# Attention with grouped queries on one core: three of 16 blocks on VectorE in every job from the tenth on

## The chip, the cores and the metric

The kernel runs on one core of a Trainium2 chip. A core has a matrix engine (TensorE, PE in the profile; its weight loads are PEld), a vector engine (VectorE, DVE), a scalar engine for activation functions (ScalarE, ACT), a general engine (GpSimd, POOL) and a queue engine (SyncE, SP). Each runs its own list of instructions in order; semaphores order them against each other. Matmuls write to PSUM, eight banks of 512 fp32 values per partition; tiles in SBUF hold the rest. The metric is the device time of one execution in microseconds (us); lower is better.

## The reference

```python
# Q [8, 512, 32, 64], K and V [8, 512, 8, 64], all fp32
scale = 1.0 / np.sqrt(dim)
K_expanded = np.repeat(K, 4, axis=2)
V_expanded = np.repeat(V, 4, axis=2)
Q, K_expanded, V_expanded = (x.transpose(0, 2, 1, 3) for x in (Q, K_expanded, V_expanded))
scores = np.einsum('bhqd,bhkd->bhqk', Q, K_expanded) * scale
weights = np.exp(scores - np.max(scores, axis=-1, keepdims=True))
weights = weights / (np.sum(weights, axis=-1, keepdims=True) + 1e-10)
output = np.einsum('bhqk,bhkd->bhqd', weights, V_expanded)
return output.transpose(0, 2, 1, 3).astype(np.float32)
```

This is attention of 8 batches, 32 query heads and 8 key heads: four query heads share one key head. Each head's 512 x 512 weights are exponentials of the scores, divided by their row sum.

## The kernel before

**Jobs.** The work is cut into 64 jobs (NJOB), one for each batch and key head, so each job has four query heads: two pairs (NPAIR = 2, index i). Two jobs make a unit u, whose Q is loaded together. The 512 keys are four chunks of 128 (kc), so a job has 2 x 4 x 2 = 16 blocks of 128 keys x 512 queries, numbered by pair, chunk and head of the pair (i, kc, m). Each block goes through scores (keys x queries, TensorE), the exponential, and a second matmul with V (P·V).

**The exponential is shared.** ScalarE does most blocks: `act_tile` takes two blocks at a time, writes their scores with two matmuls (L199) into a two-bank tile s_ps (pool s_pool, two buffers) and reads them with one ACTIVATE (L217) into pt. The other blocks are the first ones of pair 1: `taken(j)` of them, two in a normal job and three in a wide one. `act_tiles` deals the rest out: seven full tiles in a normal job; in a wide one six full tiles and, as the fifth in order (n = 4), a tile with one block, the odd block (half the size).

**The path for VectorE's blocks.** `exp_d` writes their scores into the two banks of d_ps (pool d_pool, one buffer) and VectorE turns them to 16-bit integers u (L228): the exponential's bits as a straight line. `exp_d2` takes the fraction bits f (L249), `exp_d3` computes from them a correction, g (L241) and w (L245), on GpSimd from job 3 to job 62 and on VectorE in the others, and `exp_d4` adds u and w into pt (L262; d4 for short). In a job that follows, d4 is done for the job before: u, f, g and w have two buffers. The third block of a wide job is started at the end of the job before, in the second bank of that job's d_ps tile.

**What else is in a job.** P·V for the job before (L293; `pv`), 32 small matmuls per pair into one PSUM tile pv (one buffer), in pieces between score tiles; `norm` after each pair: a reciprocal of the sums (L336, inv) and a multiply (L340, o_sb), after which pv is free again. The first reciprocal of a job (for pair 0) is called inv0, the second inv1. Eight transposes of the Q of job j + 2 on TensorE into the first bank of a d_ps tile (`trans_q`, L164), and VectorE's copy from there, qt (L167). A check of V's size (`check_v`, L173, okv) in every second job, odd ones up to batch 6 and even ones in batch 7, and a check of the sums (`check_sums`, L304) once in eight jobs. K of the next batch comes transposed through SyncE's queue; Q, K and V are loaded from GpSimd's queue, ahead of g and w in its order.

**The order is written out by hand.** Nothing is scheduled by a planner (`tc.manual_schedule()`); each engine runs its instructions in the order of the loop over j. For a job j in the steady part TensorE has: score tile 0; VectorE's two blocks; score tile 1; P·V of pair 0, 16 matmuls; score tile 2; 16 more; score tile 3; the transposes; score tile 4; P·V of pair 1 up to `cut[0]`; score tile 5; the third block of job j + 1 where that is wide; P·V up to `cut[1]`; score tile 6; the rest of P·V. VectorE has: u; okv; inv0 and multiply; qt; d4 of job j - 1; the sum check; f; u of the third block of j + 1; inv1 and multiply. P·V takes the key chunks in the order 2, 3, 1, 0, so that with three blocks taken the matmuls from the 17th on need d4.

The steps of VectorE's path as the code has them:

```python
nc.vector.tensor_scalar(out=st["u"][:, lo:hi, :], in0=ps[...], scalar1=A_U, scalar2=B_U, ...)
nc.vector.tensor_single_scalar(out=st["f"], in_=st["u"], scalar=1023, op=ALU.bitwise_and)
engine.tensor_scalar(out=g, in0=f, scalar1=-EXP_F1, scalar2=..., op0=ALU.add, op1=ALU.mult)
engine.tensor_tensor(out=w, in0=g, in1=f..., op=ALU.mult)
nc.vector.tensor_tensor(out=st["pt"]..., in0=st["u"], in1=st["w"], op=ALU.add)
```

Of the kernel before, what the change touches and what calls it, by code (L numbers as in the profile page):

```python
# [11 lines left out]
FP32 = mybir.dt.float32  # L12
# [21 lines left out]
V_HI = 1.0e15  # L34


WIDE = lambda j: j >= 10 and j % 2 == 0


@with_exitstack  # L40
# [18 lines left out]
def fast_path(ctx, tc, Q, K, V, out, flag):  # L59
    nc = tc.nc  # L60
    B, S, H, D = Q.shape
# [5 lines left out]
    NPAIR = HPG // 2  # L67
# [16 lines left out]
    s_pool = ctx.enter_context(tc.tile_pool(name="sps", bufs=2, space=PS))  # L84
# [3 lines left out]
    ident = const_pool.tile([128, 128], BF16, name="ident")  # L88
# [9 lines left out]
    kn, qn, kt, qt = {}, {}, {}, {}  # L98

    def load_k(b, lo=0, hi=KV):  # L100
        if b not in kn:
            kn[b] = knat_pool.tile([128, SC, KV, D], BF16, name="k_nat")
        nc.gpsimd.dma_start(  # L103
            out=kn[b][:, :, lo:hi, :],
            in_=K[b, :, lo:hi, :].rearrange("(sc p) g d -> p sc g d", p=128),
        )


    def load_v(b, lo=0, hi=KV, chunks=range(SC)):
        for sc in chunks:  # L110
            nc.gpsimd.dma_start(  # L111
                out=vt[b % 2][:, sc, lo:hi, 0:D],
                in_=V[b, sc * 128:(sc + 1) * 128, lo:hi, :],
            )
# [6 lines left out]
    def load_q(u, cuts=(0, 2 * HPG)):  # L121
        b, gp = divmod(u, GP)
        h0 = gp * 2 * HPG
        qn[u] = qnat_pool.tile([128, SC, 2 * HPG, D], BF16, name="q_nat")
        for lo, hi in zip(cuts[:-1], cuts[1:]):
            nc.gpsimd.dma_start(  # L126
                out=qn[u][:, :, lo:hi, :],
                in_=Q[b, :, h0 + lo:h0 + hi, :].rearrange("(sc p) h d -> p sc h d", p=128),
            )

    def d_tile():
        return d_pool.tile([128, 2, S], FP32, name="d_ps")
# [22 lines left out]
        for to, of in ((0, 64), (64, 0)):  # L155
            nc.sync.dma_start(out=kt[b][to:to + 64, 1, :, :], in_=kt[b][of:of + 64, 0, :, :])

    def trans_q(j, bank, lo=0, hi=NPAIR):
        u, g = divmod(j, 2)
        ps = bank.bitcast(BF16).rearrange("p (i sc c) -> p i sc c", i=NPAIR, sc=SC)  # L160
        for i in range(lo, hi):
            for sc in range(SC):
                h = g * HPG + 2 * i
                nc.tensor.transpose(ps[:, i, sc, :], qn[u][:, sc, h:h + 2, :], ident)  # L164
        if u not in qt:
            qt[u] = qt_pool.tile([128, 2, NPAIR, S], BF16, name="qt")
        return lambda: nc.vector.tensor_copy(  # L167
            out=qt[u][:, g, lo:hi, :], in_=ps[:, lo:hi, :, :].rearrange("p i sc c -> p i (sc c)")
        )

    def check_v(b, sc):
        n = b * SC + sc
        nc.vector.tensor_reduce(  # L173
            out=okv[:, n:n + 1], in_=vt[b % 2][:, sc, :, 0:D], op=ALU.max, axis=AX.XY,
            apply_absolute_value=True,
        )
# [6 lines left out]
    def taken(j):  # L183
        return 3 if WIDE(j) else 2

    def act_tiles(j):
        every = [(i, kc, m) for i in range(NPAIR) for kc in range(SC) for m in range(2)]
        first = DPAIR * SC * 2
        mine = [n for n in range(len(every)) if not first <= n < first + taken(j)]
        groups = [[n for n in mine if n // 2 == h] for h in range(len(every) // 2)]  # L190
        return [[every[n] for n in group] for group in groups if group]
# [3 lines left out]
    def scores(j, ps, i, kc, m):  # L195
        u, g = divmod(j, 2)
        b, gp = divmod(u, GP)
        keys = kt_first[:, gp, :, :] if b == 0 else kt[b][:, :, gp, :]
        nc.tensor.matmul(  # L199
            ps,  # L200
            keys[64 * m:64 * m + 64, g ^ m, kc * 128:(kc + 1) * 128],
            qt[u][64 * m:64 * m + 64, g, i, :],
            start=True,
            stop=True,
        )

    def open_job(j):
        pt = pt_pool.tile([128, NPAIR, SC, 2, S], FP16, name="pt")
        jobs.setdefault(j, {}).update(pt=pt, pv={})

    def act_tile(j, n):
        group = act_tiles(j)[n]
        i, kc, lo = group[0]
        ps = s_pool.tile([128, 2, S], FP32, name="s_ps")
        for _, _, m in group:
            scores(j, ps[:, m, :], i, kc, m)
        nc.scalar.activation(  # L217
            out=jobs[j]["pt"][:, i, kc, lo:, :], in_=ps[:, lo:, :], func=EXP, scale=scale
        )

    def exp_d(j, lo, hi, ps):
        st = jobs.setdefault(j, {})
        if "u" not in st:
            for name, dtype in (("u", I16), ("f", I16), ("g", BF16), ("w", BF16)):
                st[name] = dve_pool.tile([128, 3, S], dtype, name=name + "16")[:, 0:taken(j), :]
        for n in range(lo, hi):
            scores(j, ps[:, n - lo, :], DPAIR, n // 2, n % 2)
        return lambda: nc.vector.tensor_scalar(  # L228
            out=st["u"][:, lo:hi, :], in0=ps[:, 0:hi - lo, :], scalar1=A_U, scalar2=B_U,
            op0=ALU.mult, op1=ALU.add,  # L230
        )


    def by_pool(j):
        return 3 <= j < NJOB - 1
# [11 lines left out]
    def exp_d2(j):  # L247
        st = jobs[j]
        nc.vector.tensor_single_scalar(  # L249
            out=st["f"], in_=st["u"], scalar=1023, op=ALU.bitwise_and  # L250
        )
        if by_pool(j):
            exp_d3(j, nc.gpsimd)

    def exp_d3(j, engine):
        st = jobs[j]
        correction(engine, st["f"], st["g"], st["w"])
# [144 lines left out]
    bank = d_tile()  # L402
    for j in range(8):
        nc.tensor.matmul(bank[:, 1, :], warm[:, 0:128], warm, start=True, stop=True)
    for read in [first_k(0, swap, bank[:, swap, :]) for swap in range(2)]:
        read()
    bank = d_tile()
    trans_q(0, bank[:, 0, :], 0, 1)()


    for j in range(NJOB):
        end = j == NJOB - 1
        last = j - 1
        late = last >= 0
        u, g = divmod(j, 2)
        b, gp = divmod(u, GP)
        open_job(j)
        if j == 1:

            nc.gpsimd.tensor_copy(out=gate, in_=jobs[0]["pt"][0:1, 0, SC - 1, 0, 0:1])  # L420
            load_q(2)
            load_q(3)
        if g == 0 and u >= 1 and u + 3 < NU:
            load_q(u + 3)
        if (gp, g) == (1, 0) and b + 1 < B:
            load_k(b + 1)
        if 3 <= 2 * gp + g < 3 + SC and b + 1 < B:
            load_v(b + 1, chunks=(2 * gp + g - 3,))
        if gp == 2 and g == 0 and b + 1 < B:
            dma_k(b + 1)  # L430

        cut = (4, 18) if taken(j) > 2 else (11, 19)
        act_tile(j, 0)
        if j == 0:
            trans_q(0, bank[:, 1, :], 1, NPAIR)()
            act_tile(j, 1)
            exp_d(j, 0, 2, d_tile())()
        else:
            exp_d(j, 0, 2, d_tile())()
            act_tile(j, 1)  # L440

        if j == 8:
            check_v(0, 0)
        if g == (b < B - 1) and j > 1:
            check_v(b, gp)
        if late:
            pv(last, 0, 0, 16)
        act_tile(j, 2)
        if late:
            pv(last, 0, 16, 32)  # L450
            norm(last, 0)
        act_tile(j, 3)

        reads = []
        if not end:
            bank = d_tile()

            ahead = (j + 1,) if j < 7 else (8, 9) if j == 7 else (j + 2,)
            for n, to in enumerate(ahead):
                if to < NJOB:  # L460
                    reads.append(trans_q(to, bank[:, n, :]))
            if j == 1:
                for swap in range(2):
                    reads.append(first_k(1, swap, bank[:, 1, swap * S // 2:]))
            elif j > 1 and b == 0 and gp + 1 < GP:
                reads.append(first_k(gp + 1, g, bank[:, 1, :]))
        else:
            pv(j, 0, 0, 16)
        for read in reads:
            read()  # L470

        if late and by_pool(last):
            exp_d4(last)
        check_sums()
        exp_d2(j)
        if not by_pool(j):
            exp_d3(j, nc.vector)
            exp_d4(j)
        act_tile(j, 4)
        if late:  # L480
            pv(last, 1, 0, cut[0])
        act_tile(j, 5)
        if not end and taken(j + 1) > 2:
            exp_d(j + 1, 2, taken(j + 1), bank[:, 1:2, :])()
        if late:
            pv(last, 1, *cut)
        act_tile(j, 6)
        if late:
            pv(last, 1, cut[1], 32)
            norm(last, 1)  # L490
            del jobs[last]
        if end:
            pv(j, 0, 16, 32)
            norm(j, 0)
            pv(j, 1, 0, 32)
            norm(j, 1)
# [118 lines left out]
```

## Time and profile before

| what | value |
|---|---|
| median of 3 runs | 423.73 us (423.38 to 423.77) |
| span of the profiled execution, first to last instruction (no other time of it is given) | 422.0 us |
| busy share of that span: PE, PEld, DVE, ACT, POOL | 91%, 55%, 82%, 96%, 69% |
| chain that ended last: ACT, PE, DVE | 54%, 36%, 6% |
| L217, full tile, 421 of them, mean of one | 1086 ns |
| L217, odd block, 27 of them | 753 ns |
| L228, u of two blocks; of one block | 1215 ns; 685 ns |
| L249, f of two blocks; of three | 429 ns; 554 ns |
| L262, d4 of two blocks; of three | 682 ns; 949 ns |
| L241, g on POOL, two blocks; three | 1039 ns; 1466 ns |
| L245, w on POOL, two blocks; three | 2125 ns; 3095 ns |
| POOL's g waiting for DVE's f | 110.1 us, 60 times |
| granted TensorE clock, mean | 0.984 (1.00 in each stage from 20 to 400 us) |

The profile is one execution, taken by the hardware profiler. Times are microseconds from the start of the span. An instruction's duration can overlap the next one's on the same engine, so that rows are best compared by the distances between their starts. A line such as `u<-d_ps` names what is written and what is read; "idle before" and its arrow name the instruction that ended an engine's wait.

### The profile page before, as it was taken

The numbers are of one execution on the slowest core, as the hardware profiler recorded it, in microseconds if no ns is written. First come the engines' busy times: TensorE is split into PE (matmuls) and PEld (weight loads), VectorE is DVE, ScalarE is ACT, GpSimd is POOL, SyncE is SP. The second block draws the span as 40 slices with busy tenths as digits, with TensorE's granted clock in tenths as the row PEclk, the third lists the DMA queues.
The fourth block names the chain that finished last, engine by engine and source line by source line (L and its number), as shares of the span: only waits on it lengthen the run. The fifth ranks groups of instructions, "written<-read, shape, count | busy, mean of one in ns | idle before, by whom it ended". The sixth has DMA issues, their size and how long they took to land.

```text
span 422.0 us, 13063 instructions
## 1 busy us (share of the span) xinstructions
PE 385.7 (91%) x5689; PEld 233.6 (55%) x5689; DVE 344.9 (82%) x611; ACT 404.2 (96%) x449; POOL 291.8 (69%) x209
## 2 busy tenths in 40 slices
PE   6889999999999999999999999999999999999983
PEld 2446565555555555555555555555555555555552
DVE  2697788889888888888888888888989888898875
ACT  3899999999999999999999999999999999999992
POOL 8504656778758876787866887677885887666560
PEclk9599999999999999999999999999999999999998
DMA  9996986599967998499964999649996799642223
GB/s 97 177 139 159 217 165 151 70 207 187 191 151 99 216 198 160 133 198 133 229 150 116 206 163 255 157 69 200 157 225 155 122 206 207 148 123 101 102 91 115
DMA packets 91438, 66.95 MB, mean 159 GB/s; under 512 B 52080, under 2 KB 74608, under 8 KB 91376
## 3 DMA queue, kind: packets, MB, share of 16 engines
q0 software_dynamic: 56544, 25.17, 51.1%
q1 hardware_dynamic: 34832, 40.90, 34.5%
q8 instruction: 45, 0.74, 0.7%
q14 instruction: 17, 0.14, 0.1%
HBM read 50.33 MB, written 33.55 MB: 199 GB/s over the span
## 4 chain that ended last, share of the span: by engine, by line
ACT 54%; PE 36%; DVE 6%; issue 1%; POOL 1%; ACTq 0%; DVEq 0%; POOLq 0%
ACT pt L217 54%; PE s_ps L199 17%; PE pv L293 16%; PE d_ps L199 1%; DVE o_sb L340 1%; PE d_ps L164 1%; DVE pt L262 1%; DVE u L228 1%; DVE qt L167 1%; DVE w L245 0%; POOL q_nat L126 0%; DVE kt_first L146 0%; ACTq L217 0%; PE d_ps L143 0%; DVE f L249 0%
## 5 line engine op out<-in xcount | busy, mean ns | idle before, releaser
L217 ACT ACTIVATE pt<-s_ps 128x1024 f16<-128x1024 f32 (+1 forms) x448 | 402.9, 1066 | 9.1 <-PE s_ps L199 9.0
L293 PEld LDWEIGHTS <-pt 128*128 128x128 f16 x4096 | 144.2, 98 | 86.8 <-issue 50.4
L293 PE MATMUL pv<-v,pt 128*128 128x65 bf16 x4032 | 183.2, 195 | 2.6 <-DVE o_sb L340 1.6
L199 PE MATMUL s_ps<-qt,kt 64*128 64x512 bf16 x757 | 152.7, 384 | 19.9 <-ACT pt L217 15.4
L245 POOL TENSOR_TENSOR w<-g,f 128x1024 bf16<-128x1024 bf16 (+1 forms) x60 | 153.7, 2562 | 5.0
L241 POOL TENSOR_SCALAR g<-f 128x1024 bf16<-128x1024 int16 (+1 forms) x60 | 73.9, 1231 | 110.1 <-DVE f L249 110.1
L228 DVE TENSOR_SCALAR u<-d_ps 128x1024 int16<-128x1024 f32 (+1 forms) x91 | 96.2, 1058 | 1.1 <-PE d_ps L199 1.1
L340 DVE TENSOR_TENSOR o_sb<-pv,inv 128x512 f32<-128x512 f32 x125 | 86.5, 692 | 4.5 <-DVE inv L336 0.2
L199 PEld LDWEIGHTS <-kt 64*128 64x128 bf16 x896 | 49.0, 93 | 62.6 <-issue 35.0
L336 DVE RECIPROCAL inv<-pv 128x8 f32<-128x8 f32 x125 | 25.9, 207 | 55.8 <-PE pv L293 55.4
L262 DVE TENSOR_TENSOR pt<-u,w 128x1536 uint16<-128x1536 int16 (+1 forms) x64 | 50.9, 795 | 0.2
L167 DVE COPY qt<-d_ps 128x1024 bf16<-128x1024 bf16 (+1 forms) x65 | 44.3, 683 | 4.5 <-PE d_ps L164 2.9
L164 PE MATMUL d_ps<-ident,q_nat 128*128 128x128 bf16 x512 | 40.1, 222 | 1.1 <-DVE kt_first L146 0.9
L164 PEld LDWEIGHTS <-q_nat 128*128 128x128 bf16 x512 | 29.2, 98 | 15.8 <-issue 15.7
L199 PE MATMUL d_ps<-qt,kt 64*128 64x512 bf16 x139 | 31.4, 376 | 0.3
L249 DVE TENSOR_SCALAR f<-u 128x1536 int16<-128x1536 int16 (+1 forms) x64 | 30.8, 481 | 0.0
L111 POOL DMA_DIRECT2D v<-in_V_dram x32 | 29.0, 910 | 0.4 <-issue 0.4
L126 POOL DMA_DIRECT2D q_nat<-in_Q_dram x34 | 27.4, 806 | 1.5 <-DMA q_nat<-in_Q_dram 1.3
L199 PE MATMUL s_ps<-qt,kt_first 64*128 64x512 bf16 x112 | 23.7, 419 | 4.1 <-ACT pt L217 3.0
L173 DVE TENSOR_REDUCE okv<-v 128x1 f32<-128x512 bf16 x32 | 21.6, 675 | 0.0
L199 PEld LDWEIGHTS <-kt_first 64*128 64x128 bf16 x128 | 8.0, 95 | 12.2 <-issue 8.4
L103 POOL DMA_DIRECT2D k_nat<-in_K_dram x10 | 7.7, 770 | 1.0 <-POOLq L599 0.8
(40 smaller groups left out, 37.6 us busy)
## 6 DMA issues: line engine op xcount, KB each, us to landing
out_dram<-o_sb SPq DMA_DIRECT2D x31, 1024.0 KB, 6.9
q_nat<-in_Q_dram POOLq DMA_DIRECT2D x31, 512.0 KB, 6.3
k_nat<-in_K_dram POOLq DMA_DIRECT2D x7, 512.0 KB, 8.6
v<-in_V_dram POOLq DMA_DIRECT2D x28, 128.0 KB, 7.6
kt<-kt SPq DMA_DIRECT2D x14, 256.0 KB, 4.6
out_dram<-o_sb SPq DMA_DIRECT2D x4, 256.0 KB, 2.4
kt<-k_nat SPq DMA_TRANSPOSE x28, 5.6
v<-in_V_dram POOLq DMA_DIRECT2D x4, 96.0 KB, 7.8
```

What stands on the lines that cost most here:

```text
L111: nc.gpsimd.dma_start(out=vt[b % 2][:, sc, lo:hi, 0:D], in_=V[b, sc * 128:(sc + 1) * 128, lo:hi, :],)
L164: nc.tensor.transpose(ps[:, i, sc, :], qn[u][:, sc, h:h + 2, :], ident)
L167: return lambda: nc.vector.tensor_copy(out=qt[u][:, g, lo:hi, :], in_=ps[:, lo:hi, :, :].rearrange("p i sc c -> p i (sc c)"))
L199: nc.tensor.matmul(ps, keys[64 * m:64 * m + 64, g ^ m, kc * 128:(kc + 1) * 128], qt[u][64 * m:64 * m + 64, g, i, :], start=True, stop=True,)
L217: nc.scalar.activation(out=jobs[j]["pt"][:, i, kc, lo:, :], in_=ps[:, lo:, :], func=EXP, scale=scale)
L228: return lambda: nc.vector.tensor_scalar(out=st["u"][:, lo:hi, :], in0=ps[:, 0:hi - lo, :], scalar1=A_U, scalar2=B_U, op0=ALU.mult, op1=AL ...
L241: engine.tensor_scalar(out=g, in0=f, scalar1=-EXP_F1, scalar2=EXP_K * 2.0 ** (24 * as_bits), op0=ALU.add, op1=ALU.mult,)
L245: engine.tensor_tensor(out=w, in0=g, in1=f.bitcast(FP16) if as_bits else f, op=ALU.mult)
L249: nc.vector.tensor_single_scalar(out=st["f"], in_=st["u"], scalar=1023, op=ALU.bitwise_and)
L262: nc.vector.tensor_tensor(out=st["pt"][:, DPAIR, :, :, :].rearrange("p kc m q -> p (kc m) q")[:, 0:n, :].bitcast(U16), in0=st["u"], in1=st ...
L293: nc.tensor.matmul(st["pv"][i][:, m, qc, :], st["pt"][:, i, kc, m, qc * 128:(qc + 1) * 128], vt[b % 2][:, kc, 2 * gp + g, :], start=(n < 2 ...
L340: nc.vector.tensor_tensor(out=osb[u][:, :, h:h + 2, :].rearrange("p qc m d -> p m qc d"), in0=sums[:, :, :, 0:D], in1=inv[:, :, :, None].t ...
```

## The change

Every job from 9 to 62 is wide (before: the even ones from 10 on). The odd block of a wide job is written to the second bank of the d_ps tile whose first bank takes the transposes, just ahead of them, in place of a tile of s_pool; ScalarE reads it there. `apart` declares that the transposes, and the copy qt, don't depend on that read, as they are in the other bank. `exp_d2`, with g and w behind it on GpSimd, is issued right after score tile 1, so that f follows u on VectorE. The cut of pair 1's P·V is at 0 and 16. The third block of job j + 1 comes after score tile 6.

```diff
-WIDE = lambda j: j >= 10 and j % 2 == 0
+WIDE = lambda j: 9 <= j < 63
...
+    def apart(this, other):
+        if other is not None:
+            tc.declare_no_dep(
+                this.ins, other.ins, reason="the two are in different banks of one tile"
+            )
+        return this
+
-    def trans_q(j, bank, lo=0, hi=NPAIR):
+    def trans_q(j, bank, lo=0, hi=NPAIR, other=None):
...
-                nc.tensor.transpose(ps[:, i, sc, :], qn[u][:, sc, h:h + 2, :], ident)
+                apart(
+                    nc.tensor.transpose(ps[:, i, sc, :], qn[u][:, sc, h:h + 2, :], ident), other
+                )
...
-        return lambda: nc.vector.tensor_copy(
+        return lambda: apart(nc.vector.tensor_copy(
             out=qt[u][:, g, lo:hi, :], in_=ps[:, lo:hi, :, :].rearrange("p i sc c -> p i (sc c)")
-        )
+        ), other)
...
-    def act_tile(j, n):
+    def act_tile(j, n, spare=None):
         group = act_tiles(j)[n]
         i, kc, lo = group[0]
-        ps = s_pool.tile([128, 2, S], FP32, name="s_ps")
+        ps = s_pool.tile([128, 2, S], FP32, name="s_ps") if spare is None else spare
...
-        nc.scalar.activation(
+        return nc.scalar.activation(
...
-        cut = (4, 18) if taken(j) > 2 else (11, 19)
+        cut = (0, 16) if taken(j) > 2 else (11, 19)
...
             act_tile(j, 1)
+        exp_d2(j)
...
             bank = d_tile()
+            beside = act_tile(j, 4, bank) if taken(j) > 2 else None
...
-                    reads.append(trans_q(to, bank[:, n, :]))
+                    reads.append(trans_q(to, bank[:, n, :], other=beside))
...
         check_sums()
-        exp_d2(j)
         if not by_pool(j):
             exp_d3(j, nc.vector)
             exp_d4(j)
-        act_tile(j, 4)
+        if taken(j) == 2:
+            act_tile(j, 4)
         if late:
             pv(last, 1, 0, cut[0])
         act_tile(j, 5)
-        if not end and taken(j + 1) > 2:
-            exp_d(j + 1, 2, taken(j + 1), bank[:, 1:2, :])()
         if late:
             pv(last, 1, *cut)
         act_tile(j, 6)
+        if not end and taken(j + 1) > 2:
+            exp_d(j + 1, 2, taken(j + 1), bank[:, 1:2, :])()
         if late:
             pv(last, 1, cut[1], 32)
```

## The prediction

> **What bounds the kernel now.** I read the busy time by stage first, then the order of time on VectorE, GpSimd and TensorE over one pair of jobs, then an instruction that a neighbour lengthened.
>
> ```profile
> core 0: us, PE busy (x) PEld busy (x) DVE busy (x) ACT busy (x) POOL busy (x), PEclk, DMA share, GB/s
> 20.00:40.00 20.00, 17.58 (x278) 11.11 (x276) 16.38 (x31) 18.61 (x21) 3.77 (x3) 1.00 0.86 165
> 200.00:240.00 40.00, 37.65 (x567) 22.75 (x565) 34.20 (x60) 40.00 (x46) 30.40 (x20) 1.00 0.83 179
> ```
>
> From 40 to 400 us ScalarE is busy 40.00 of every 40.00 us at full granted clock; it is the bound. Two jobs, one wide (13 blocks on ScalarE) and one normal (14), take 12.50 us: the reciprocals at 207.02 and 219.52 below. Two normal jobs take 12.84 us (the f of L249 starts at 67.71 and 80.55), so a normal job is 6.42 and a wide one 12.50 - 6.42 = 6.08.
>
> VectorE over those two jobs (start, duration, instruction):
>
> ```profile
> 207.02 0.21 DVE L336 RECIPROCAL inv<-pv 128x8 f32<-128x8 f32 x1 [0.91 <-PE pv L293]
> 207.26 0.69 DVE L340 TENSOR_TENSOR o_sb<-pv,inv 128x512 f32<-128x512 f32 x1
> 207.87 1.22 DVE L228 TENSOR_SCALAR u<-d_ps 128x1024 int16<-128x1024 f32 x1
> 209.00 0.68 DVE L173 TENSOR_REDUCE okv<-v 128x1 f32<-128x512 bf16 x1
> 209.62 0.21 DVE L336 RECIPROCAL inv<-pv 128x8 f32<-128x8 f32 x1
> 209.86 0.69 DVE L340 TENSOR_TENSOR o_sb<-pv,inv 128x512 f32<-128x512 f32 x1
> 210.49 0.69 DVE L167 COPY qt<-d_ps 128x1024 bf16<-128x1024 bf16 x1
> 211.10 0.95 DVE L262 TENSOR_TENSOR pt<-u,w 128x1536 uint16<-128x1536 int16 x1
> 211.97 0.42 DVE L249 TENSOR_SCALAR f<-u 128x1024 int16<-128x1024 int16 x1
> ...
> 215.98 0.21 DVE L336 RECIPROCAL inv<-pv 128x8 f32<-128x8 f32 x1 [0.68 <-PE pv L293]
> ...
> 219.52 0.21 DVE L336 RECIPROCAL inv<-pv 128x8 f32<-128x8 f32 x1 [0.91 <-PE pv L293]
> ```
>
> GpSimd in the same stretch:
>
> ```profile
> 206.21 1.47 POOL L241 TENSOR_SCALAR g<-f 128x1536 bf16<-128x1536 int16 x1 [1.32 <-DVE f L249]
> 207.76 3.10 POOL L245 TENSOR_TENSOR w<-g,f 128x1536 bf16<-128x1536 bf16 x1
> 212.48 1.04 POOL L241 TENSOR_SCALAR g<-f 128x1024 bf16<-128x1024 int16 x1 [1.62 <-DVE f L249]
> ```
>
> TensorE:
>
> ```profile
> 208.01 0.66 PE L293 MATMUL pv<-v,pt 128*128 128x65 bf16 x16
> 208.60 0.39 PE L199 MATMUL s_ps<-qt,kt 64*128 64x512 bf16 x2
> 208.92 0.66 PE L293 MATMUL pv<-v,pt 128*128 128x65 bf16 x16
> ```
>
> What to see: the wide w runs from 207.76 to 210.86, and d4 (L262, the add of u and w into pt) starts at 211.10, after it; f follows d4, and only then does GpSimd start again. Comparing all starts and ends in the trace, none of the 64 d4 and none of the 64 f overlaps a g or a w on GpSimd. What does lie beside g and w on VectorE are u, the reciprocals, the multiplies, qt and okv, and all keep their durations (okv 674 to 678 ns, beside w in 31 of 32 cases).
>
> One VectorE instruction of this family was lengthened by GpSimd, at the start:
>
> ```profile
> 12.78 0.71 DVE L249 TENSOR_SCALAR f<-u 128x1024 int16<-128x1024 int16 x1
> ```
>
> It is the only such f not at 0.42 us, and GpSimd was issuing a Q load from 12.51 to 13.27: 0.29 us late. A d4 beside such an issue, in contrast, kept its 0.95 us (86.09, with a V load issued 85.80 to 86.75).
>
> **The change, part by part.** I set the clock of a job to 0 at the reciprocal that closes the job before (inv1).
>
> *ScalarE* gives one more block in 27 odd jobs: 6.42 - 6.08 = 0.34 us each, 9.2 us, if nothing else becomes the bound.
>
> *VectorE* gets in those 27 jobs u of one block (0.69), f 0.42 to 0.55, d4 0.68 to 0.95: 1.09 us by the rows, about 1.0 as start-to-start. A pair had 34.20/40 x 12.50 = 10.7 us of work; 11.7 is still under 12.2, so not a bound by sum, but its order is now the chain. The steps, each a distance between starts in the rows above: inv1 to multiply 0.24, to u 0.61; u to f, which now reads u right behind it, 1.22 + 0.03 (the gap before a dependent instruction, as from reciprocal to multiply); f to the next 0.47; okv 0.62; reciprocal to multiply 0.24, to qt 0.63, to d4 0.61.
> - Job with okv (the V check; odd jobs up to batch 7): f 2.10, okv 2.57, inv0 3.19, multiply 3.43, qt 4.06, d4 wanted at 4.67.
> - Job without it: TensorE decides. P·V of pair 0 starts 0.05 after the multiply ends (207.95 to 208.01): 0.98; 16 matmuls 0.59, a score tile 0.32, second half 1.89; inv0 0.70 later (215.28 to 215.98) 2.59; second half to score tile 0.59, odd-block score 0.21, transposes 0.31 later at 3.00; they take 0.62 and qt starts 0.04 behind: 3.66; d4 wanted at 4.27.
>
> *Behind d4* stands the second half of pair 1's P·V: with the cut at 16 it begins with a block that d4 writes. d4 0.95, 0.05 to the first matmul, 0.70 to the next inv1: + 1.70. u of the third block (0.69, ready about 0.45 after its matmul) fits inside. So undisturbed the jobs take 4.67 + 1.70 = 6.37 and 5.97, a pair 12.34: above ScalarE's 12.16, a little under today's 12.50.
>
> *f moved up* is the other half. GpSimd's g starts 0.65 after f does, w 1.55 after g: f at 2.10, g 2.75, w 4.30 to 7.40. It moves past no queue that waits on it (loads of Q, K and V stand ahead of g in GpSimd's order as before, 0.8 to 0.9 each, and GpSimd is free for them from 7.40 on). But it takes w from behind the previous d4 to right over it. In the kernel before, w ended 0.24 ahead of d4; now d4 of job j-1 is wanted at 4.67 or 4.27 while w of job j holds 4.30 to 7.40.
>
> No row shows a d4 beside a w. The bounds: it costs nothing (0.95, as beside a V load), or d4 waits until w is through. Nearest is the lengthened f, a VectorE instruction that reads and writes SBUF alone and that GpSimd's access held back; and d4 beside a load issue is no test, for that reads no tensor. I take the upper end. Then d4 runs 7.40 to 8.35, and the job ends at 9.10, wherever w is first. With okv that is every job (4.67 against 4.30). Without it d4 and w want to start within 0.03 us of each other, closer than these rows carry: where d4 is first the job stays 5.97, w slips behind d4 (5.22 to 8.32), the next f is held to 2.35, and its job is 9.35.
>
> The Trainium skill states this mechanism ("SBUF — State Buffer", section "Who interferes with whom"): VectorE's second SBUF port is GpSimd's own, a VectorE instruction with two SBUF inputs contends with a GpSimd one that reads SBUF, and the later one blocks for the whole instruction. The lengthened f and the untouched d4 beside a load agree with it; d4 beside w is what no run here shows yet.
>
> *The odd block's scores in the second bank* free a score buffer slot for TensorE (the 0.3 us waits of its score tiles for ScalarE); *transposes not waiting for that read* keep qt where I put it; the third block's matmul does wait for ScalarE's read and for qt, both done by about 5 in the undisturbed job. Their worth is inside the 5.97 and 6.37, no extra term.
>
> *Jobs 4 to 8* are normal, but f moves there too: f 2.10, g 2.61, w 3.73 to 5.86, d4 5.86 to 6.54, the rest of the P·V behind it (19 matmuls left of which 5 wait, a score tile, 13 more) to inv1 at about 7.7: 1.3 us over 6.42, five jobs, + 6.5.
> *Start and end*: in jobs 1 and 2 f (0.45) leaves the chain f, g, w, d4 on VectorE that delays a multiply and ScalarE twice, and in the last job the same before the last d4: - 1.2 at best, 0 at worst; I take - 1.2. The sum check (L304, 0.61, seven times) sits behind d4 and adds 0.3 each: + 2.
>
> **Sum**, on the span of 422.0 (the median of runs, 423.73, is 1.7 longer; I carry that over). All 54 wide jobs at 9.10: 54 x (9.10 - 6.25) = 154, + 6.5 + 2 - 1.2 = + 161: 585. Every job without okv escaping: 27 x (9.35 + 5.97 - 12.50) = 76, + 7.3 = + 83: 507. As d4 and w are that close, I put half of them each way: 546.
>
> **The rivals.**
> 1. *They share*: d4 beside w takes about twice 0.95. Then an okv job is 7.3, the others 5.97: 27 x 0.79 = 21, + 2 + about 4 in the jobs before the tenth: 450. For it: nothing shows a wait of 3 us. Against: the f was held by 0.29 us of a 0.76 us issue, as by a holder, not by half speed.
> 2. *No exclusion*, the other side: a pair 12.34, 27 x -0.16 = -4.3, + 2, - 1.2: 420.2. It decides where d4 keeps 0.95 beside w. For it: okv and the rest run beside w untouched. Against: these have at most one large SBUF tensor, and the order of the kernel before keeps d4 and f clear of g and w. A delay of 0.13 us in each pair would already make this no change.
> 3. *The transposes wait for ScalarE after all*, so that the change isn't what it says: that read ends at about 4.6 of the job (four tiles of 6.42/7 = 0.92 from about 0.4 on, then half a tile), the transposes would start there instead of at 3.00, and d4 1.2 us later even in the okv job: without exclusion 54 x 1.2 = 65, 485. The instructions as built carry no wait on ScalarE ahead of the transposes; 0.03.
>
> **Chances.** Waiting out w 0.62 (507 to 585), sharing 0.13, no exclusion 0.20, the third 0.03, worse than all 0.02. The range leaves out no exclusion and the far tails: 440 to 590. A measurement of this kernel tells 0.2% (0.85 us) from no change; no exclusion splits into faster 0.16 and same 0.03, and some of its spread is slower: faster 0.16, same 0.03, slower 0.81.
>
> **What would show it.** d4's row: 0.95 beside w, or starts that sit at the ends of w, or spans of 2 to 4 us (a held instruction may show as a long one, like the f). The spacing of jobs by okv parity: 9.1 and 6.0, 9.1 and 9.1, or 6.37 and 5.97. ScalarE's busy share falls to about 6.1 of 7.5 to 9.1 us, with its idle time put down to PE scores, and PE's to d4. I am wrong if ScalarE stays at 40.00 of 40.00.

## The result and the profile after

| what | before | after |
|---|---|---|
| median (all executions) | 423.56 us (423.24 to 423.77, 4) | 541.5 us (531.75, 533.28, 549.73, 563.85) |
| ratio, 95% interval | | 1.257 [1.254, 1.2599] |
| span of the profiled execution | 422.0 us | 530.0 us (531.75 us in all) |
| granted TensorE clock, mean | 0.984 | 0.908 |
| ScalarE busy, share of the span | 96% | 76% |

The ratio is taken over the executions at 531.75 and 533.28; the two longer ones (granted clock 0.88) are left out of it as disturbed, and no profile shows them.

The stretch from 200 to 240 us after the change, by windows (busy us of PE, PEld, DVE, ACT, POOL; then the granted clock, DMA share, GB/s):

```profile
core 0: us, PE busy (x) PEld busy (x) DVE busy (x) ACT busy (x) POOL busy (x), PEclk, DMA share, GB/s
200.00:240.00 40.00, 30.00 (x424) 17.05 (x422) 36.48 (x48) 29.34 (x35) 26.06 (x15) 0.91 0.68 113
```

ScalarE's 40.00 of 40.00 has become 29.34. VectorE shows 36.48, more than its 34.20 of before, but with 48 instructions in place of 60: its instructions have become longer, not more. The page's chain and groups say which:

```profile
DVE 58%; PE 36%; issue 3%; ACT 1%; POOL 1%; DVEq 0%; ACTq 0%; POOLq 0%
...
L226 ACT ACTIVATE pt<-s_ps 128x1024 f16<-128x1024 f32 x394 | 380.3, 1038 | 121.1 <-issue 86.4
L302 PE MATMUL pv<-v,pt 128*128 128x65 bf16 x4032 | 188.1, 204 | 110.3 <-DVE pt L271 94.7
...
L271 DVE TENSOR_TENSOR pt<-u,w 128x1536 uint16<-128x1536 int16 (+1 forms) x64 | 143.9, 2248 | 0.1
```

The chain that ended last has moved from ScalarE (54%) to VectorE (58%), and d4, L271, took 143.9 us where it took 50.9 before. TensorE stands 94.7 us in front of it, and ScalarE's idle time ahead of its full tiles has gone from 9.1 to 121.1 us. Note the last column of d4's group: 0.1 us idle before it. The wait is inside its span. The d4 of three blocks alone, which took 949 ns before:

```profile
L271 DVE TENSOR_TENSOR pt<-u,w 128x1536 uint16<-128x1536 int16 x54 | 129.1, 2390 | 0.0
```

Four jobs in a row, VectorE (the reciprocals named are the last ones of their jobs):

```profile
205.34 0.21 DVE L345 RECIPROCAL inv<-pv 128x8 f32<-128x8 f32 x1
...
207.44 0.56 DVE L258 TENSOR_SCALAR f<-u 128x1536 int16<-128x1536 int16 x1
...
209.95 3.59 DVE L271 TENSOR_TENSOR pt<-u,w 128x1536 uint16<-128x1536 int16 x1
...
214.59 0.20 DVE L345 RECIPROCAL inv<-pv 128x8 f32<-128x8 f32 x1
...
219.78 3.01 DVE L271 TENSOR_TENSOR pt<-u,w 128x1536 uint16<-128x1536 int16 x1
...
223.56 0.21 DVE L345 RECIPROCAL inv<-pv 128x8 f32<-128x8 f32 x1
...
229.24 2.54 DVE L271 TENSOR_TENSOR pt<-u,w 128x1536 uint16<-128x1536 int16 x1
...
232.53 0.21 DVE L345 RECIPROCAL inv<-pv 128x8 f32<-128x8 f32 x1
...
236.84 0.95 DVE L271 TENSOR_TENSOR pt<-u,w 128x1536 uint16<-128x1536 int16 x1
...
238.56 0.21 DVE L345 RECIPROCAL inv<-pv 128x8 f32<-128x8 f32 x1
```

GpSimd in the same stretch:

```profile
208.09 1.47 POOL L250 TENSOR_SCALAR g<-f 128x1536 bf16<-128x1536 int16 x1 [4.33 <-DVE f L258]
209.65 3.08 POOL L254 TENSOR_TENSOR w<-g,f 128x1536 bf16<-128x1536 bf16 x1
...
218.89 3.09 POOL L254 TENSOR_TENSOR w<-g,f 128x1536 bf16<-128x1536 bf16 x1
...
227.86 3.10 POOL L254 TENSOR_TENSOR w<-g,f 128x1536 bf16<-128x1536 bf16 x1
...
236.83 3.92 POOL L254 TENSOR_TENSOR w<-g,f 128x1536 bf16<-128x1536 bf16 x1
```

Lay one over the other. The first w ends at 209.65 + 3.08 = 212.73, and the first d4 at 209.95 + 3.59 = 213.54: 0.81 later, a little under its own free length. The second and third pairs give 221.98 and 222.79, 230.96 and 231.78: 0.81 and 0.82. The w is in each case that of the next job, which this d4 doesn't read. Wherever d4 starts in w, it ends 0.8 us after w does: 0.80 to 0.82 in all 35 of the 54 that w holds. The fourth pair starts within 0.01 us; d4 keeps its 0.95, and it is w that has grown, from 3.09 to 3.92. So one waits out the other, and the profiler shows the wait as a longer instruction. The distances of the reciprocals are 9.25, 8.97, 8.97 and 6.03 us.

### The profile page after: what moved, and what is told of

It is laid out like the page before. It is cut to its first block, busy times and chain, and to the rows that moved or that the text cites. A ratio compares the mean times of both kernels' runs of the same rounds, so it can differ in the third digit from the quotient of the medians.

```text
span 530.0 us, 13074 instructions
## 1 busy us (share of the span) xinstructions
PE 402.8 (76%) x5689; PEld 235.2 (44%) x5689; DVE 469.4 (89%) x638; ACT 400.7 (76%) x449; POOL 342.5 (65%) x209
## 4 chain that ended last, share of the span: by engine, by line
DVE 58%; PE 36%; issue 3%; ACT 1%; POOL 1%; DVEq 0%; ACTq 0%; POOLq 0%
DVE pt L271 26%; PE pv L302 17%; PE s_ps L208 10%; DVE o_sb L349 9%; DVE u L237 9%; DVE qt L176 7%; PE d_ps L172 4%; PE d_ps L208 4%; DVE inv L345 2%; ACT pt L226 1%; DVE f L258 1%; DVE ok L313 1%; DVE kt_first L146 0%; DVE okv L182 0%; DVE w L254 0%
## 5 line engine op out<-in xcount | busy, mean ns | idle before, releaser
L226 ACT ACTIVATE pt<-s_ps 128x1024 f16<-128x1024 f32 x394 | 380.3, 1038 | 121.1 <-issue 86.4
L302 PE MATMUL pv<-v,pt 128*128 128x65 bf16 x4032 | 188.1, 204 | 110.3 <-DVE pt L271 94.7
L302 PEld LDWEIGHTS <-pt 128*128 128x128 f16 x4096 | 156.2, 104 | 208.9 <-DVE pt L271 121.1
L254 POOL TENSOR_TENSOR w<-g,f 128x1536 bf16<-128x1536 bf16 (+1 forms) x60 | 192.2, 3203 | 5.0
L250 POOL TENSOR_SCALAR g<-f 128x1536 bf16<-128x1536 int16 (+1 forms) x60 | 85.5, 1426 | 166.8 <-DVE f L258 166.1
L208 PE MATMUL s_ps<-qt,kt 64*128 64x512 bf16 x676 | 144.0, 422 | 0.5 <-ACT pt L226 0.4
L271 DVE TENSOR_TENSOR pt<-u,w 128x1536 uint16<-128x1536 int16 (+1 forms) x64 | 143.9, 2248 | 0.1
L237 DVE TENSOR_SCALAR u<-d_ps 128x1024 int16<-128x1024 f32 x118 | 115.1, 976 | 6.3 <-PE d_ps L208 1.1
L208 PE MATMUL d_ps<-qt,kt 64*128 64x512 bf16 x220 | 67.3, 415 | 3.7 <-DVE u L237 3.4
L208 PEld LDWEIGHTS <-kt 64*128 64x128 bf16 x896 | 38.9, 95 | 34.0 <-issue 10.6
L226 ACT ACTIVATE pt<-d_ps 128x512 f16<-128x512 f32 x54 | 33.1, 613 | 0.0
```

The source lines that it names most:

```text
L208: nc.tensor.matmul(ps, keys[64 * m:64 * m + 64, g ^ m, kc * 128:(kc + 1) * 128], qt[u][64 * m:64 * m + 64, g, i, :], start=True, stop=True,)
L226: return nc.scalar.activation(out=jobs[j]["pt"][:, i, kc, lo:, :], in_=ps[:, lo:, :], func=EXP, scale=scale)
L237: return lambda: nc.vector.tensor_scalar(out=st["u"][:, lo:hi, :], in0=ps[:, 0:hi - lo, :], scalar1=A_U, scalar2=B_U, op0=ALU.mult, op1=AL ...
L254: engine.tensor_tensor(out=w, in0=g, in1=f.bitcast(FP16) if as_bits else f, op=ALU.mult)
L271: nc.vector.tensor_tensor(out=st["pt"][:, DPAIR, :, :, :].rearrange("p kc m q -> p (kc m) q")[:, 0:n, :].bitcast(U16), in0=st["u"], in1=st ...
L302: nc.tensor.matmul(st["pv"][i][:, m, qc, :], st["pt"][:, i, kc, m, qc * 128:(qc + 1) * 128], vt[b % 2][:, kc, 2 * gp + g, :], start=(n < 2 ...
```

## The experiments

The first four were run on one chip, beside a kernel before of 423.34 us (422.94 to 424.62); the next four on another, beside 424.13 (423.35 to 424.93); the last beside 423.76 (423.21 to 424.93).

### f back behind d4, all else of the change kept

```diff
             act_tile(j, 1)
-        exp_d2(j)
...
         check_sums()
+        exp_d2(j)
```

> The changed kernel with f (and g, w behind it) put back behind d4; everything else of the change stays, 54 wide jobs included. Exclusion theory: f, g, w run as a loop d4 0.87, f 0.55, g 1.47, w 3.10 and gaps 0.2, so d4 is next wanted when w is through; no d4 over 1.0 us in the steady part, a job 6.2 to 6.8 us (more where two loads are issued on GpSimd), 430 to 440 us. Rival (the longer chain: more VectorE work, the odd block in the second bank, the cut): all of that is still here, so it stays above 500 us.

Measured: 433.2 us (432.19 to 433.6), ratio 1.0225 [1.0199, 1.0251]. Its three-block d4 (by shape; busy us and mean ns, then the idle time before it) and the busy times from 200 to 240 us:

```profile
L271 DVE TENSOR_TENSOR pt<-u,w 128x1536 uint16<-128x1536 int16 x54 | 51.4, 952 | 6.0 <-POOL w L254 6.0
```
```profile
200.00:240.00 40.00, 35.51 (x548) 20.24 (x544) 36.21 (x62) 38.12 (x44) 34.19 (x19) 1.00 0.89 158
```

All 54 are back at 0.95 us. Against 532.5 us, the mean of the two executions in the ratio above, moving this one call is worth 99 us of the 109 lost. What stays is 10 us over the kernel before, and the line points to the reason: d4 now stands idle for w (6.0 us in all), which it didn't before. The run with every job wide, below, takes this up.

### f moved up alone, in the kernel before

```diff
         else:
             exp_d(j, 0, 2, d_tile())()
             act_tile(j, 1)
+        exp_d2(j)
...
         check_sums()
-        exp_d2(j)
```

> The kernel before with only f moved up behind u; even jobs wide as before. Exclusion theory: in the odd jobs d4 of three blocks is wanted at 4.7 us of the job beside a w at 3.7 to 5.9 us, and waits; odd jobs 8.0 to 8.5, even ones about 6.1; 470 to 500 us, and d4 stretched in odd jobs. Rival (the longer chain): f in front of the first reciprocal costs 0.25 us in odd jobs, about 431 us, no stretched d4.

Measured: 491.65 us (488.1 to 493.12), ratio 1.1622 [1.1582, 1.1661]. By shape:

```profile
L262 DVE TENSOR_TENSOR pt<-u,w 128x1536 uint16<-128x1536 int16 x27 | 57.5, 2129 | 0.0
```

The move does its harm without any of the other parts. In jobs with the V check 26 of 27 d4 are lengthened. In the others it is 10 of 27, in jobs of up to 8.47 us, which the expectation had missed: it put these at 6.1 throughout.

### No g and w on GpSimd

```diff
-        if by_pool(j):
-            exp_d3(j, nc.gpsimd)
...
-            in1=st["w"],
+            in1=st["f"].bitcast(BF16) if by_pool(j) else st["w"],
```

For jobs 3 to 62 this leaves out the correction of the exponential; d4 adds f's bits in w's place, with the same shape and types.

> The changed kernel without g and w on GpSimd (jobs 3 to 62): the correction is left out, d4 adds f's bits, read as bf16, in place of w, with the same shape and engine; all else is as in the changed kernel. Exclusion theory: the undisturbed chain, 12.34 us a pair, 419 to 423 us, every d4 at 0.95. Rival (the longer chain): unchanged above 500 us.

Measured: 419.5 us (418.73 to 419.96), ratio 0.99 [0.9876, 0.9925].

```profile
L269 DVE TENSOR_TENSOR pt<-u,f 128x1536 uint16<-128x1536 int16 x54 | 51.2, 948 | 0.0
```

With no g and w on GpSimd, d4 is 0.95 everywhere, and the jobs between 200 and 240 us alternate between 6.02 and 6.31 us (6.60 where the sum check falls). The rest of the change does what it says, and it would gain 1%.

### w in three instructions, one for each block

```diff
-        engine.tensor_tensor(out=w, in0=g, in1=f.bitcast(FP16) if as_bits else f, op=ALU.mult)
+        f = f.bitcast(FP16) if as_bits else f
+        if not as_bits:
+            engine.tensor_tensor(out=w, in0=g, in1=f, op=ALU.mult)
+            return
+        for n in range(f.shape[1]):
+            engine.tensor_tensor(out=w[:, n, :], in0=g[:, n, :], in1=f[:, n, :], op=ALU.mult)
```

> The changed kernel with w as one GpSimd instruction for each block (three of about 1.1 us in place of one of 3.1). Exclusion for a whole instruction: d4 waits for the end of one such piece, not for the last, so that it is at most about 2.1 us long (now up to 3.6), a job 6.1 to 7.9, 450 to 490 us. Exclusion until GpSimd has nothing more queued: d4 up to 4 us, 540 us or more. Sharing in proportion: d4 lasts as long as before the split, about 535 us.

Measured: 474.93 us (473.5 to 475.28), ratio 1.1208 [1.1177, 1.1238]. VectorE by shape, and one f from its timeline:

```profile
L276 DVE TENSOR_TENSOR pt<-u,w 128x1536 uint16<-128x1536 int16 x54 | 76.7, 1420 | 0.0
L263 DVE TENSOR_SCALAR f<-u 128x1536 int16<-128x1536 int16 x54 | 35.7, 662 | 1.9
```
```profile
223.20 0.81 DVE L263 TENSOR_SCALAR f<-u 128x1536 int16<-128x1536 int16 x1
```

A d4 now waits for the piece that it meets and not for the whole: 1.42 us in the mean in place of 2.39, 2.18 at most (there it met a whole g). A wait shared by halves would not care how w is cut. The f, 0.56 us when free, also waits out a piece: 0.81. So it isn't d4 alone.

### Work for TensorE while it stands

```diff
+        if taken(j) > 2 and g == (b < B - 1):
+            idle = s_pool.tile([128, 2, S], FP32, name="s_ps")
+            for n in range(8):
+                nc.tensor.matmul(idle[:, n % 2, :], warm[:, 0:128], warm, start=True, stop=True)
```

Eight matmuls whose result nobody reads, ahead of the P·V that waits for d4, in the jobs with the V check. This tests something that the trace of after shows and the prediction had not: the granted clock falls to half after a long stand (last section), TensorE's work of the next job gets slower, and the next d4 is wanted later, when w has already begun. Jobs without the V check are then held too often.

> The changed kernel with eight matmuls on a constant tile (128 x 512, read by nobody) on TensorE right before the matmul that waits for d4, in the jobs with the V check only. Clock theory: in the changed kernel TensorE's 2.9 us stand at d4 is followed by some 3.4 us at half the granted clock, which makes the next job's d4 be wanted 0.9 us later, behind the start of w, so that it is held too; with the stand partly filled the clock stays at 1.00 there, the next d4 comes level with w and gets in front more often: granted clock over 0.97, 500 to 522 us. Rival (the half clock costs nothing, as that d4 would be held anyway): 525 us or more, as many held d4 as before.

Measured: 526.59 us in the median (509.76, 525.84, 527.34, 530.52), above the range of the clock theory. In the profiled execution, the one of 509.76, the clock is 0.967, seven stretches of half clock are left of 23, and of the d4 in jobs without the V check 5 of 27 are held in place of 19; in the jobs with it 19 of 27 in place of 21. That one is as the clock theory has it (its clock just short of the 0.97 expected). But the five held d4 start 0.017 to 0.020 us behind w, and one that starts 0.016 behind it escapes, so that the count hangs on hundredths of a microsecond. One execution shows that a filled stand brings d4 level with w; what this is worth isn't settled.

### The changed kernel again

> The changed kernel once more, for its spread (531.75 to 563.85 in four executions). If the spread comes from how many d4 of jobs without the V check are held, another profile of another length has another count of long d4, at some 3 us each; if it comes from the clock alone, the count is the same (46 of the 54 wide ones over 1.0 us, or so) and the granted clock differs.

Measured: 543.86 us (530.74, 531.1, 556.63, 564.66), ratio 1.2523 [1.2492, 1.2554]. The profiled execution, the one of 530.74, has the same 21 and 19 held d4 and 23 stretches of half clock as that of 531.75. An execution of another length wasn't profiled, so neither reading of the expectation is decided.

### Every job wide, nothing else

```diff
-WIDE = lambda j: j >= 10 and j % 2 == 0
+WIDE = lambda j: 9 <= j < 63
```

> The kernel before with all jobs from 9 to 62 wide and nothing else of the change (f behind d4, odd block in a tile of its own, the old cut). Exclusion theory: the loop d4, f, g, w (6.2 us, 6.8 with two loads issued) sets the job as with f put back, 430 to 437 us, no d4 over 1.0 us; so the second bank and the new cut are worth under 4 us here. Rival (these edits carry the gain): 445 us or more.

Measured: 432.75 us (432.38 to 433.67), ratio 1.0211 [1.0191, 1.0231], the same as with f moved back (433.2). So in the old order the second bank and the new cut bring nothing, and a loop between two engines bounds the job. From its timeline, VectorE and then GpSimd:

```profile
214.69 0.96 DVE L262 TENSOR_TENSOR pt<-u,w 128x1536 uint16<-128x1536 int16 x1 [0.35 <-POOL w L245]
215.57 0.55 DVE L249 TENSOR_SCALAR f<-u 128x1536 int16<-128x1536 int16 x1
```
```profile
216.21 1.47 POOL L241 TENSOR_SCALAR g<-f 128x1536 bf16<-128x1536 int16 x1 [1.55 <-DVE f L249]
217.77 3.10 POOL L245 TENSOR_TENSOR w<-g,f 128x1536 bf16<-128x1536 bf16 x1
```

d4 to f 0.88, f to g 0.64, g to w 1.56, w 3.10, and 0.06 to the next d4 at 220.93: 6.24 us for one turn, and the loads that GpSimd issues ahead of a g come on top where they meet it. The 54 wide jobs take 6.42 us in the mean; ScalarE's 13 blocks would take 6.08.

### One buffer for w

```diff
+    w_pool = ctx.enter_context(tc.tile_pool(name="w", bufs=1))
...
-                st[name] = dve_pool.tile([128, 3, S], dtype, name=name + "16")[:, 0:taken(j), :]
+                pool = w_pool if name == "w" else dve_pool
+                st[name] = pool.tile([128, 3, S], dtype, name=name + "16")[:, 0:taken(j), :]
```

Now w has to wait until the d4 of the job before has read the old one: a wait more, which puts d4 first every time.

> The changed kernel with one buffer for w in place of two, so that w of a job can't start before d4 of the job before has read it. Exclusion, decided by who starts first: d4 always comes first, none over about 2.2 us (it can still meet g), w starts behind it; jobs 6.0 to 7.4 us, 440 to 465 us although a wait was added. Rival (d4 is slow for another reason): 535 us or more.

Measured: 471.58 us (469.96 to 472.09), ratio 1.1117 [1.1092, 1.1142]. An added wait saves 61 us (against 532.5). No d4 of a job with the V check is held; in the others 18 of 27 meet g, which has no such wait. But the time is 6.6 us above the range. The timeline of VectorE in a job with a sum check shows what was forgotten:

```profile
243.91 0.95 DVE L273 TENSOR_TENSOR pt<-u,w 128x1536 uint16<-128x1536 int16 x1
244.78 3.46 DVE L315 SCALAR_TENSOR_TENSOR ok<-inv,ok 128x128 f32<-128x128 f32 x2
248.16 0.68 DVE L239 TENSOR_SCALAR u<-d_ps 128x512 int16<-128x512 f32 x1
```

d4 goes first, lets w go (245.01 to 248.09), and the sum check behind d4, two instructions of 0.29 us with both inputs in SBUF, waits w out in its place.

### One buffer for w, sum check ahead of d4

Beside the edit above:

```diff
+        check_sums()
         if late and by_pool(last):
             exp_d4(last)
-        check_sums()
```

> w in one buffer again, and the sum check moved ahead of d4. In the run of w in one buffer six jobs with a sum check took 9.70 us or thereabouts in place of 6.55, with the check's row at 3.46 us while w ran, and the job behind each took 7.9 in place of 6.4 to 7.3, partly at a lower granted clock. If that is the check (two inputs in SBUF) waiting out w like d4, these jobs now take 6.55 + 0.6 and the ones behind them 6.4 to 7.3: 6 x 2.5 + 6 x 1.0 = 21 us less than 471.6, so 445 to 456, the check's rows at 0.29 us, and at most 3 windows of half clock. If the length came from something else in these jobs (the loads of the next unit, w's wait itself), the time stays at 466 to 474.

Measured: 451.62 us (450.42 to 452.38), ratio 1.0662 [1.0635, 1.0688]. The sum check by shape:

```profile
L315 DVE SCALAR_TENSOR_TENSOR ok<-inv,ok 128x128 f32<-128x128 f32 x14 | 4.0, 288 | 0.2
```

14 instructions take 4.0 us where they took 21.1 with the check behind d4. Its jobs take 7.08 in place of 9.70, those behind them 7.1 in place of 7.4 to 8.1, and from 40 to 430 us the clock is granted in full. That accounts for the miss. What the trace shows to be left over: in the jobs without the V check 23 of 27 d4 meet a g (up to 2.20 us), and the f of three blocks takes 0.81 us in place of 0.56, as it waits out the end of w:

```profile
L273 DVE TENSOR_TENSOR pt<-u,w 128x1536 uint16<-128x1536 int16 x54 | 74.3, 1376 | 0.0
L260 DVE TENSOR_SCALAR f<-u 128x1536 int16<-128x1536 int16 x54 | 43.7, 809 | 1.8
```

No kernel here that computes the whole is faster than the one before.

## Why the prediction was right

*d4 waits until w is through*: the step on which everything hung, taken from one f that was 0.29 us late. Right: moving f alone brings the waits (491.65), moving it back or taking GpSimd's reads away removes them (433.2, 419.5), and cutting w shortens them (474.93). The Trainium skill's rule ("SBUF — State Buffer", section "Who interferes with whom") that the later of the two blocks for the whole of the other is what these traces show: d4 up to 3.60 us, w 3.92 where it was the later.

*The clock of a job*: d4 wanted at 4.67 after inv1 with the V check, 4.27 without. In the trace 209.95 - 205.34 = 4.61 and 236.84 - 232.53 = 4.31. Undisturbed jobs of 6.37 and 5.97 were forecast; the run without g and w has 6.31 and 6.02, and its 419.5 stands beside the 420.2 of the rival without exclusion. A held job was put at 9.10; the 37 long ones of the 54 wide jobs average 9.08. A plain one is 8.97, as d4 ends 0.81 behind w and not 0.95.

*Half of the jobs without the V check escape*: near in its effect, and that by luck, for the working was not right. Where TensorE runs at full clock and w isn't late, d4 and w tie as worked out, but in this profile it is no even chance: d4 goes first all seven times (it starts from 0.006 us ahead of w to 0.013 behind). Two things were missed, of opposite sign.

First, such a job keeps its 4.31 only at full clock. Behind a long stand it runs at half clock for a while, and d4 is wanted at 5.0 to 5.9, well behind w's start: at 219.78, 5.19 behind the reciprocal and 0.89 behind w's start. This holds 14 of the 27, and 5 more meet a g (below), so that 19 are lengthened and not half.

Second, the job behind an escape was to be held at 9.35, because w, put behind d4, would hold the next f. VectorE and GpSimd behind the escape at 236.84:

```profile
240.65 0.56 DVE L258 TENSOR_SCALAR f<-u 128x1536 int16<-128x1536 int16 x1
...
243.16 0.95 DVE L271 TENSOR_TENSOR pt<-u,w 128x1536 uint16<-128x1536 int16 x1
...
249.18 1.90 DVE L271 TENSOR_TENSOR pt<-u,w 128x1536 uint16<-128x1536 int16 x1
...
256.45 3.60 DVE L271 TENSOR_TENSOR pt<-u,w 128x1536 uint16<-128x1536 int16 x1
```
```profile
240.70 1.00 POOL L111 DMA_DIRECT2D v<-in_V_dram  x1
241.78 1.46 POOL L250 TENSOR_SCALAR g<-f 128x1536 bf16<-128x1536 int16 x1
243.33 3.74 POOL L254 TENSOR_TENSOR w<-g,f 128x1536 bf16<-128x1536 bf16 x1
247.02 0.82 POOL L126 DMA_DIRECT2D q_nat<-in_Q_dram  x1
247.85 0.89 POOL L111 DMA_DIRECT2D v<-in_V_dram  x1
248.81 1.47 POOL L250 TENSOR_SCALAR g<-f 128x1536 bf16<-128x1536 int16 x1
250.36 3.68 POOL L254 TENSOR_TENSOR w<-g,f 128x1536 bf16<-128x1536 bf16 x1
...
256.15 3.09 POOL L254 TENSOR_TENSOR w<-g,f 128x1536 bf16<-128x1536 bf16 x1
```

f is not held (w ends 0.10 after it starts), and a V load of 1.00 us, which the prediction had put into idle time, stands between w and g. It moves w to 0.17 behind the next d4, which escapes too; the one after meets only g and loses 0.95; then GpSimd has caught up and d4 is held again. An escape is thus worth three short jobs (6.03, 6.31, 6.98) and not one. So it goes in five of the eight escapes; the one at 138.67 has no load ahead of the next g, and the next job is held. The one at 468.96 gains nothing, since the sum check behind d4 waits w out (3.50 us for its two instructions): its job takes 9.19. With 19 lengthened the first would have raised the time, and this lowers it: 37 long jobs, where half escaping had meant 40.

*The sum*, on the span: the 54 wide jobs took 106.6 us more than before, where half way between 154 and 76, with 2 for the sum check, gives 117. Jobs 4 to 8 took 34.86 in place of 32.17: 2.7, where 6.5 was forecast. The wait itself came as worked out (in job 5 w ends at 5.88 and d4 at 6.42, forecast 5.86 and 6.54). The P·V behind it was put too high: only 8 matmuls wait for a d4 of two blocks, and the reciprocal starts 0.51 behind d4, where the forecast had 1.2. Start and end: - 1.3 against - 1.2. Together 108.0 against 122.3, and 531.75 for the profiled execution against 546. That the median of the four, 541.5, lies nearer is luck, for the sum knows of no spread between executions.

*The rivals.* Sharing (450): out, since a span that ends 0.8 us behind w wherever it began is a wait and not a lower speed. No exclusion: out by the same lines. The transposes waiting for ScalarE: out, as qt and d4 stand where the working put them. ScalarE's gain of 9.2 us exists only in the run without g and w, and there 4 us of it.

## What to carry to other kernels

When GpSimd helps VectorE, look at which instructions of the two may lie side by side, not only at their dependences: in the kernel before, an order that looked like slack kept d4, f and the sum check clear of g and w, and an order that starts the helper earlier cost 25%. Look for the cost inside durations: compare the mean of a shape across two profiles before reading the waits. Where overlap can't be avoided, a wait that puts the short instruction first, or a long one cut in pieces, takes back much of it (1.257 of the time before to 1.066 and 1.121).

## What the hardware showed that was not expected

*The granted clock.* TensorE in the jobs above:

```profile
213.60 0.66 PE L302 MATMUL pv<-v,pt 128*128 128x65 bf16 x16 [2.91 <-DVE pt L271]
214.20 0.61 PE L208 MATMUL s_ps<-qt,kt 64*128 64x512 bf16 x2
...
215.69 1.06 PE L302 MATMUL pv<-v,pt 128*128 128x65 bf16 x16
...
217.98 0.39 PE L208 MATMUL s_ps<-qt,kt 64*128 64x512 bf16 x2
```

In each profile the changes of the granted clock stand whole multiples of 3.413 us apart. By windows of that length, the stand and what follows (busy time of PE, then the clock):

```profile
core 0: us, PE busy (x), PEclk, DMA share, GB/s
210.78:214.19 3.41, 0.59 (x16) 1.00 0.00 0
214.19:217.60 3.41, 3.41 (x34) 0.50 1.13 156
217.60:221.01 3.41, 3.00 (x45) 1.00 0.96 151
```

TensorE stands 2.9 us with the clock still at 1.00; shortly after it resumes, the clock is at half, a pair of score matmuls takes 0.61 us in place of 0.39 and 16 of the P·V 1.06 in place of 0.66. There are 23 stretches at half clock after 40 us, and one before the change. Apart from the last one, at the end of the program, they are 3.41 us long, four of them twice that. In this profile all 21 stands of 2.11 us and more behind d4 were followed by one, and none of the 20 from 1.15 to 2.08. The length of the stand isn't all, though: with f moved up alone, 8 of 23 stands of 1.4 us were followed by one too, and in the last run, whose stands reach 1.4, none was.

What the whole window held separates them better. Over all eleven profiles, from 40 us on, each of the 60 windows at full clock in which TensorE was busy for less than 1.7 us was followed by one at half clock, and none of the 1140 with more than 2.03 us was; of the 62 between, 21 were. So a stand of 1.4 us counts or not by how it falls into the windows. No run changed this alone.

The Trainium skill ("TensorE: Matmul & The Clock Gate", Part 1) has a half clock behind an idle window of about 3.4 us that runs free of the work. The half and the 3.41 us agree, and so does the fixed grid; an idle window wasn't needed here, a stand well under one was enough.

*How close is a tie.* Over all runs, a d4 that starts up to 0.016 us behind w's recorded start still goes first; one that starts 0.017 or more behind it is held. A d4 that begins with 0.08 us of g left isn't lengthened, one with 0.21 left by 0.06.
